# Other places in the on-chip memory for the split weights of a decoder trunk, with four tiles of each part in place of five

## The chip, the core and the metric

The kernel runs on one core of one Trainium2 chip. The metric is the device time of one execution, in microseconds; the span is the part of it that the profile covers. The engines are named as the profile names them: PE (TensorE, matrix products; PEld is its weight load), DVE (VectorE), ACT (ScalarE), POOL (GpSimd), SP (SyncE, which here issues nearly all transfers).

## What is computed

A trunk of two layers over 256 tokens of width 2048: first a pooling mixer, then 16-head attention, each followed by a gated feed-forward block of inner width 5632 with a causal convolution of three taps. Everything is float32, and nearly all of the arithmetic is `x @ W` with large matrices.

```python
for i in range(DEPTH):
    mod = cond @ w_ada[i] + b_ada[i]
    sh1, sc1, g1, sh2, sc2, g2 = jnp.split(mod, 6, axis=-1)
    h = modulate(rmsnorm(x, norm_g[i, 0]), sh1, sc1)
    y = pool_mixer(...) if i % N_MIXERS == 0 else moba_attention(h, w_qkv[li], w_o[li], rel_table)
    x = x + g1[:, None, :] * y
    h = modulate(rmsnorm(x, norm_g[i, 1]), sh2, sc2)
    x = x + g2[:, None, :] * conv_ffn(h, w_up[i], conv_w[i], conv_b[i], w_down[i])
return rmsnorm(x, final_g)
```

## The kernel before

**Steps and halves.** The matrices `w_up`, `w_down`, `w_qkv` and `w_o` are worked off in 328 steps (list `steps`). A step is a block of 512 rows by 512 columns: one transfer of 1 MB brings it into a raw tile of 128 partitions by 4 x 512 floats (`w_load`, five raw tiles). Each step has two halves of two 128-row blocks, 656 halves in all; half (133, 0) is the first half of step 133.

**The split.** Every half is split in two parts that PE can multiply in one pass (type float32r). ACT copies the raw half into the first part `hi` with rounding, then DVE writes the rest, raw minus `hi`, into the second part `lo` (`w_use`). The activations are split in the same way (tile `h` and the `act` and `o` tiles: first 256 columns rounded, next 256 the rest). A product then takes three matmuls of 256 columns for each 128 x 128 block of weights: `hi` with both parts of `h`, `lo` with the first. That is 24 matmuls for a half and 48 for a step; `v` alone multiplies the other way round, with the weights as the moving operand of 512 columns, 12 for a half.

**What sets how far the split runs ahead.** There are HB = 5 tiles for `hi` and 5 for `lo`. The split of a half is written into the program LAG = 3 halves ahead of its products: after it, the list `pending` is longer than LAG and `run_half` writes the products of the oldest half, with the side work that hangs on them.

```python
ac.activation(hi, src, AF.Copy)
ve.tensor_tensor(lo, src, hi.bitcast(F32), op=ALU.subtract)
pending.append((i, half) + ...)
if len(pending) > LAG:
    run_half()
```

A half can be split when its two tiles are free, that is when PE is through with the half that had them before. In the last step of every group, and in all steps of the first ten groups of layer 0 (which add each step's result to a tile in the on-chip memory, `home`), the products of both halves are written together, block by block, so both halves of the step stay occupied until its end.

**Order.** The first 200 of the loads and their uses are put in order on each engine by a scheduler, by priorities; from there on the engines run in the order in which the program was written. The conditioning products (`accs`, `acc`: DVE adds of raw tiles `ws`, `wa`) share DVE and the five raw tiles with the steps. At about 200 us the first step begins; what lies before is conditioning and the pooling mixer. Near 960 us and 1355 us a norm needs the whole of `x` before the next product can start.

**Places.** The tiles lie in the order in which the pools were made: constants, then `raw`, `hi`, `lo`, then the work pool. The tile `starts` is 48 floats long so that what follows begins 64 bytes past a multiple of 128. `h` begins at byte 36,864 of a partition, a multiple of 1024, and so do the tiles `act`, `o` and `pw`. Places modulo 1024 as built:

| tiles | before | after the change |
|---|---|---|
| raw, 5 of 8192 B | 960 each | 0 each |
| hi | 960 in all 5 | 64, 192, 320, 448 |
| lo | 960 in all 5 | 576, 704, 832, 960 |
| h, act, o, pw | 0 | 0 |

One 128-column block of a weight tile is 512 bytes, so from one column block to the next the place moves between 960 and 448 before.

Of the kernel before, what the change touches and what calls it, by code (L numbers as in the profile page):

```python
# [9 lines left out]
F32 = mybir.dt.float32  # L10
F32R = mybir.dt.float32r
# [6 lines left out]
P = 128  # L18
# [3 lines left out]
BUCKETS = 32  # L22
# [3 lines left out]
def bucket_starts():  # L26

    exact = BUCKETS // 2

    def bucket(n):  # L30
        if n < exact:
            return n
        big = exact + int(math.log(n / exact) / math.log(MAX_DIST / exact) * (BUCKETS - exact) + 1e-9)
        return min(big, BUCKETS - 1)

    of = [bucket(n) for n in range(4 * MAX_DIST)]
    return [next((n for n, b in enumerate(of) if b >= want), 1 << 20) for want in range(BUCKETS)]
# [19 lines left out]
def trunk(ctx: ExitStack, tc: tile.TileContext, x, c, norm_g, w_ada, b_ada, pool_w, pool_scale, w_qkv, w_o,  # L57
# [3 lines left out]
    _, S, D = x.shape  # L61
# [4 lines left out]
    H = rel_table.shape[1]  # L66
    NT = S // P
    SCALE = float(P) ** -0.5
    C = 512
# [3 lines left out]
    const = ctx.enter_context(tc.tile_pool(name="const", bufs=1))  # L73
    wp = ctx.enter_context(tc.tile_pool(name="wp", bufs=1))
# [2 lines left out]
    dram = ctx.enter_context(tc.tile_pool(name="dram", bufs=1, space=bass.MemoryType.DRAM))  # L77

    PE_BLOCKS = ((2, 5, 8, 11, 14), (3, 7, 11, 15), (2, 4, 6, 9, 11, 13, 15), (2, 5, 7, 10, 13, 15), ())
    RAW, HB, LAG, T4, PRIO = 5, 5, 3, 6, 1000  # L80

    def raw_tile(name):
        return wp.tile([P, 4 * C], F32, tag="raw", name=name, bufs=RAW)
# [4 lines left out]
    def aux(name):  # L88
        return psum.tile([P, C], F32, tag="aux", name=name, bufs=2)

    def wt(shape, tag, bufs, name, dt=F32):
        return work.tile(shape, dt, tag=tag, bufs=bufs, name=name)

    rel = wt([BUCKETS, H], "rel", 1, "rel")


    ident = const.tile([P, P], F32, name="ident")
# [570 lines left out]
    def bias_rows():  # L668

        starts = bucket_starts() + [1 << 20]  # L670
        st = const.tile([P, 48], F32, name="starts")[:, :BUCKETS + 1]
        for b, v in enumerate(starts):
            nc.gpsimd.memset(st[:, b:b + 1], float(v))
        nc.gpsimd.dma_start(rel, rel_table)
        e = wt([H, S + P], "t4", T4, "bias_e")
        nc.gpsimd.memset(e, NEG)
        for t in range(NT):
            ni = wt([P, 1], "st", 8, f"ni{t}", I32)
            nc.gpsimd.iota(ni, pattern=[[0, 1]], base=t * P, channel_multiplier=1)
            n = wt([P, 1], "st", 8, f"nf{t}")  # L680
            ve.tensor_copy(n, ni)
            ge = wt([P, BUCKETS + 1], "oh", 2, f"ge{t}")
            ve.tensor_scalar(ge, st, n, None, op0=ALU.is_le)
            oh = wt([P, BUCKETS + 1], "oh", 2, f"oh{t}")
            ve.tensor_tensor(oh[:, :BUCKETS], ge[:, :BUCKETS], ge[:, 1:], op=ALU.subtract)
            ps = aux(f"ohp{t}")
            pe.transpose(ps[:BUCKETS, :P], oh[:, :BUCKETS], ident)
            ohT = wt([BUCKETS, P], "vec", 4, f"ohT{t}")
            ve.tensor_copy(ohT, ps[:BUCKETS, :P])
            ps2 = aux(f"ohe{t}")  # L690
            pe.matmul(ps2[:H, :P], rel, ohT, start=True, stop=True)
            ve.tensor_copy(e[:, P - 1 + t * P:P - 1 + (t + 1) * P], ps2[:H, :P])
        nc.gpsimd.dma_start(bias_dram, e)
# [273 lines left out]
    def run_half():  # L967
        i, half, hi, lo = pending.pop(0)
        steps[i][3](half, hi, lo)
        if half == 1:  # L970
            for f in hooks.get(i, ()):
                f()
        h_next = ahead.pop(0) if ahead else None
        if h_next:
            h_next()
        else:
            run_tasks(2 if len(tasks) > MANY else 1)
        for _ in range(2):
            if folds:
                folds.pop(0)()  # L980
        for d in list(deferred):
            d[0] -= 1
            if d[0] <= 0:
                deferred.remove(d)
                d[1]()

    def w_use(i):
        def use(r):
            for half in range(2):
                hi = wp.tile([P, 2 * C], F32R, tag="hi", name=f"hi{i}_{half}", bufs=HB)  # L990
                lo = wp.tile([P, 2 * C], F32R, tag="lo", name=f"lo{i}_{half}", bufs=HB)
                src = r[:, half * 2 * C:(half + 1) * 2 * C]
                ac.activation(hi, src, AF.Copy)
                ve.tensor_tensor(lo, src, hi.bitcast(F32), op=ALU.subtract)
                pending.append((i, half) + tuple(t.rearrange("p (k c) -> p k c", k=2) for t in (hi, lo)))
                if len(pending) > LAG:
                    run_half()
        return use
# [47 lines left out]
    i = 0  # L1046
# [86 lines left out]
```

## Time and profile before

| | us |
|---|---|
| time, median of 3 runs (lowest to highest) | 2121.81 (2120.65 to 2122.86) |
| the profiled execution's own time | 2123.99 |
| its span | 2121.9 |
| PE busy in the span | 2066.2 |
| DVE busy | 1643.3 |
| ACT busy | 959.2 |

The profile is of one execution of its own, which took 2.18 us more than the median of the runs. Busy times overlap. A PE instruction counts as busy from its start to the modelled end of its pipeline, so instructions that follow each other overlap too, and the distance from start to start is what a matmul costs. Names of tiles stand without their numbers, so a row `lo<-w,hi` can be any half; which one it is follows from the engine's order. All compute instructions show line 50, a helper that records them; they are told apart by tiles.

### The profile page before, as it was taken

What the parts mean: (1) busy time and instruction counts of PE and PEld (TensorE: products, weight loads), DVE (VectorE), ACT (ScalarE), POOL (GpSimd) and SP (SyncE); (2) the same over time, 40 slices, a digit from 0 to 9 for tenths busy, and PEclk for the clock granted to TensorE, in tenths of its full rate; (3) what the DMA queues carried; (4) which work ended last, traced back from release to release, by engine and by line L of the source; (5) the groups of instructions that cost most, each with busy time, mean ns of one, the idle gap of its engine ahead of it and who ended that gap; (6) DMA issues with size and microseconds to landing.
All of it is one profiled execution on the core that took longest, in us unless ns stands there. A gap on an engine that the chain in (4) does not pass through costs nothing.

```text
span 2121.9 us, 38504 instructions
## 1 busy us (share of the span) xinstructions
PE 2066.2 (97%) x16292; PEld 1963.9 (93%) x16292; DVE 1643.3 (77%) x2023; ACT 959.2 (45%) x1206; POOL 12.0 (1%) x64
## 2 busy tenths in 40 slices
PE   6888999999999999999999999999999999999998
PEld 2435999999999999999999999999999999999998
DVE  6877799799879998997787878779775666556655
ACT  3113633566354445444544444445443454434443
POOL 1000000000000000000000000000000000000000
PEclk9889999999999999999999999999999999999999
DMA  9999999565998988896888888578765555555551
GB/s 357 333 348 345 335 334 320 198 197 181 348 332 292 358 314 308 304 326 213 307 294 310 295 310 302 190 259 282 278 233 179 190 179 189 196 180 188 192 179 60
DMA packets 236445, 558.78 MB, mean 263 GB/s; under 512 B 9272, under 2 KB 9592, under 8 KB 221680
## 3 DMA queue, kind: packets, MB, share of 16 engines
q1 hardware_dynamic: 234800, 553.17, 74.5%
q8 instruction: 127, 2.08, 0.4%
q0 software_dynamic: 896, 2.49, 0.4%
q10 hardware_dynamic: 576, 0.67, 0.1%
q14 instruction: 46, 0.38, 0.0%
HBM read 554.17 MB, written 2.12 MB: 262 GB/s over the span
## 4 chain that ended last, share of the span: by engine, by line
PE 95%; DVE 2%; DMA 2%; ACT 1%; issue 1%; ACTq 0%; SPq 0%; DVEq 0%
PE uv L50 24%; PE ug L50 23%; PE d L50 23%; PE k L50 4%; PE wo L50 4%; PE q L50 4%; PE v L50 4%; PE row L50 2%; PE pp L50 2%; PE mods L50 1%; DVE accs L50 1%; DVE pool_room L50 1%; DMA w<-in_w_up_dram 1%; DMA ws<-in_w_ada_dram 1%; PE sc L50 0%
## 5 line engine op out<-in xcount | busy, mean ns | idle before, releaser
L50 DVE TENSOR_TENSOR lo<-w,hi 128x1024 fp32r<-128x1024 f32 x656 | 793.9, 1222 | 320.7 <-ACT hi L50 319.7
L50 ACT ACTIVATE hi<-w 128x1024 fp32r<-128x1024 f32 x656 | 682.3, 1057 | 671.9 <-PE d L50 215.8
L50 PE MATMUL uv<-h,hi 128*128 128x256 f32 x2816 | 503.8, 281 | 4.2 <-ACT h L50 4.1
L50 PE MATMUL ug<-h,hi 128*128 128x256 f32 x2816 | 501.6, 280 | 0.2 <-ACT hi L50 0.2
L50 PE MATMUL d<-act,hi 128*128 128x256 f32 x2816 | 497.5, 280 | 0.0
L50 PEld LDWEIGHTS uv<-h,hi 128*128 128x128 f32 x2816 | 433.2, 189 | 5.2 <-ACT h L50 4.9
L50 PEld LDWEIGHTS ug<-h,hi 128*128 128x128 f32 x2816 | 431.3, 188 | 0.5 <-ACT hi L50 0.5
L50 PEld LDWEIGHTS d<-act,hi 128*128 128x128 f32 x2816 | 428.9, 187 | 0.0
L50 PE MATMUL uv<-h,lo 128*128 128x256 f32 x1408 | 394.1, 280 | 0.0
L50 PE MATMUL ug<-h,lo 128*128 128x256 f32 x1408 | 393.2, 279 | 0.0
L50 PE MATMUL d<-act,lo 128*128 128x256 f32 x1408 | 390.9, 279 | 0.0
L50 PEld LDWEIGHTS uv<-h,lo 128*128 128x128 f32 x1408 | 265.8, 189 | 0.0
L50 PEld LDWEIGHTS ug<-h,lo 128*128 128x128 f32 x1408 | 264.8, 188 | 0.0
L50 PEld LDWEIGHTS d<-act,lo 128*128 128x128 f32 x1408 | 263.5, 188 | 0.0
L50 DVE SCALAR_TENSOR_TENSOR acc<-wa,cond,acc 128x2048 f32<-128x2048 f32 x105 | 246.3, 2346 | 3.5 <-DMA wa<-in_w_ada_dram 3.3
L50 DVE SCALAR_TENSOR_TENSOR accs<-ws,cond,accs 128x512 f32<-128x512 f32 (+1 forms) x179 | 157.4, 882 | 23.3 <-DMA ws<-in_w_ada_dram 12.5
L50 PE MATMUL k<-h,hi 128*128 128x256 f32 x512 | 94.0, 285 | 1.1 <-ACT h L50 1.1
L50 PE MATMUL q<-h,hi 128*128 128x256 f32 x512 | 91.4, 280 | 0.0
L50 PE MATMUL wo<-o,hi 128*128 128x256 f32 x512 | 91.1, 280 | 0.0
L50 PE MATMUL row<-ws,cond 128*1 128x512 f32 x152 | 79.5, 647 | 10.3 <-DMA ws<-in_w_ada_dram 10.3
L50 PEld LDWEIGHTS k<-h,hi 128*128 128x128 f32 x512 | 79.9, 190 | 2.3 <-ACT h L50 1.4
L50 PE MATMUL v<-hi,h 128*128 128x512 f32 x256 | 80.4, 395 | 0.0
(157 smaller groups left out, 1751.7 us busy)
## 6 DMA issues: line engine op xcount, KB each, us to landing
w<-in_w_up_dram SPq DMA_DIRECT2D x176, 1024.0 KB, 5.2
wa<-in_w_ada_dram SPq DMA_DIRECT2D x112, 1024.0 KB, 6.0
w<-in_w_down_dram SPq DMA_DIRECT2D x88, 1024.0 KB, 5.1
ws<-in_w_ada_dram SPq DMA_DIRECT2D x56, 1024.0 KB, 9.0
w<-in_w_qkv_dram SPq DMA_DIRECT2D x48, 1024.0 KB, 5.9
ws<-in_w_ada_dram SPq DMA_DIRECT2D x48, 512.0 KB, 5.8
w<-in_w_o_dram SPq DMA_DIRECT2D x16, 1024.0 KB, 5.3
pw<-in_pool_w_dram SPq DMA_DIRECT2D x4, 1024.0 KB, 9.1
```

The lines of the kernel that those rows point to most:

```text
L50: ins = call(*args, **kwargs)
```

## The change

The tiles `hi` and `lo` get 32 floats more (4224 bytes instead of 4096), and the data lie 16 floats (64 bytes) into them. HB goes from 5 to 4 and LAG from 3 to 2. The small tile `rel` moves from the work pool to the constants, and `starts` is no longer padded; by that the raw tiles begin on a multiple of 1024, and the work pool keeps its places modulo 1024.

```diff
--- before.py
+++ after.py
@@ -77,7 +77,7 @@
     dram = ctx.enter_context(tc.tile_pool(name="dram", bufs=1, space=bass.MemoryType.DRAM))
 
     PE_BLOCKS = ((2, 5, 8, 11, 14), (3, 7, 11, 15), (2, 4, 6, 9, 11, 13, 15), (2, 5, 7, 10, 13, 15), ())
-    RAW, HB, LAG, T4, PRIO = 5, 5, 3, 6, 1000
+    RAW, HB, LAG, T4, PRIO = 5, 4, 2, 6, 1000
 
     def raw_tile(name):
         return wp.tile([P, 4 * C], F32, tag="raw", name=name, bufs=RAW)
@@ -90,8 +90,6 @@
 
     def wt(shape, tag, bufs, name, dt=F32):
         return work.tile(shape, dt, tag=tag, bufs=bufs, name=name)
-
-    rel = wt([BUCKETS, H], "rel", 1, "rel")
 
 
     ident = const.tile([P, P], F32, name="ident")
@@ -668,9 +666,10 @@
     def bias_rows():
 
         starts = bucket_starts() + [1 << 20]
-        st = const.tile([P, 48], F32, name="starts")[:, :BUCKETS + 1]
+        st = const.tile([P, BUCKETS + 1], F32, name="starts")
         for b, v in enumerate(starts):
             nc.gpsimd.memset(st[:, b:b + 1], float(v))
+        rel = const.tile([BUCKETS, H + 8], F32, name="rel")[:, :H]
         nc.gpsimd.dma_start(rel, rel_table)
         e = wt([H, S + P], "t4", T4, "bias_e")
         nc.gpsimd.memset(e, NEG)
@@ -987,8 +986,9 @@
     def w_use(i):
         def use(r):
             for half in range(2):
-                hi = wp.tile([P, 2 * C], F32R, tag="hi", name=f"hi{i}_{half}", bufs=HB)
-                lo = wp.tile([P, 2 * C], F32R, tag="lo", name=f"lo{i}_{half}", bufs=HB)
+
+                hi, lo = (wp.tile([P, 2 * C + 32], F32R, tag=w, name=f"{w}{i}_{half}", bufs=HB)[:, 16:16 + 2 * C]
+                          for w in ("hi", "lo"))
                 src = r[:, half * 2 * C:(half + 1) * 2 * C]
                 ac.activation(hi, src, AF.Copy)
                 ve.tensor_tensor(lo, src, hi.bitcast(F32), op=ALU.subtract)
```

The same instructions are issued on every engine; SP's and POOL's stand in the same order as before. On ACT, DVE and, in the scheduled part, PE the order changes, as at these places.

**DVE in the up products of layer 0, steps 13 to 15 (`home`: a product's result added to its tile; `accs`: conditioning).** Before, the piece from the second split of step 13 to the first of step 15 reads on DVE:

```order
L50 TENSOR_TENSOR lo13_1_1927<-w13_1720,hi13_1_1926 128x1024
L50 TENSOR_TENSOR lo14_0_1942<-w14_1831,hi14_0_1941 128x1024
L50 TENSOR_TENSOR home0_1178<-home0_1178,ug0_0_0_1930 128x512
L50 SCALAR_TENSOR_TENSOR accs_207<-ws3_2_3_1867,cond_95,accs_207 128x1024 x2
L50 TENSOR_TENSOR home0_1178<-home0_1178,ug0_0_1_1931 128x512
L50 TENSOR_TENSOR lo14_1_1994<-w14_1831,hi14_1_1993 128x1024
L50 TENSOR_TENSOR lo15_0_2009<-w15_1872,hi15_0_2008 128x1024
```

Now the piece from the first split of step 13 to the second of step 14 reads on DVE:

```order
L50 TENSOR_TENSOR lo13_0_1923<-w13_1768,hi13_0_1922 128x1024
L50 TENSOR_TENSOR lo13_1_1931<-w13_1768,hi13_1_1930 128x1024
L50 TENSOR_TENSOR home0_1174<-home0_1174,ug0_0_0_1926 128x512
L50 SCALAR_TENSOR_TENSOR accs_206<-ws3_2_3_1915,cond_94,accs_206 128x1024 x2
L50 TENSOR_TENSOR home0_1174<-home0_1174,ug0_0_1_1927 128x512
L50 TENSOR_TENSOR lo14_0_1990<-w14_1855,hi14_0_1989 128x1024
L50 TENSOR_TENSOR lo14_1_1998<-w14_1855,hi14_1_1997 128x1024
```

The pair of splits between two steps' additions was the second half of one step and the first of the next, and is now both halves of one step.

**DVE at the first norm of layer 1 (`ht` and `h1_0` make the new activations; step 132 is the first of the attention).** Before, the activations 4 to 7 of the norm stand like this on DVE:

```order
L50 SCALAR_TENSOR_TENSOR ht10_4_9921<-xT_101,gsc_115,rrow_9901 128x256
L50 SCALAR_TENSOR_TENSOR ht10_5_9924<-xT_101,gsc_115,rrow_9901 128x256
L50 SCALAR_TENSOR_TENSOR h1_0_9904<-ht10_4_9921,mod_114,h1_0_9904 128x256
L50 SCALAR_TENSOR_TENSOR h1_0_9904<-ht10_5_9924,mod_114,h1_0_9904 128x256
L50 TENSOR_TENSOR lo133_1_9930<-w133_9546,hi133_1_9929 128x1024
L50 TENSOR_TENSOR lo134_0_9962<-w134_9619,hi134_0_9961 128x1024
L50 SCALAR_TENSOR_TENSOR ht10_6_9989<-xT_101,gsc_115,rrow_9901 128x256
L50 SCALAR_TENSOR_TENSOR ht10_7_9992<-xT_101,gsc_115,rrow_9901 128x256
L50 SCALAR_TENSOR_TENSOR h1_0_9904<-ht10_6_9989,mod_114,h1_0_9904 128x256
L50 SCALAR_TENSOR_TENSOR h1_0_9904<-ht10_7_9992,mod_114,h1_0_9904 128x256
L50 TENSOR_TENSOR lo134_1_9998<-w134_9619,hi134_1_9997 128x1024
```

Now the same activations stand like this on DVE:

```order
L50 SCALAR_TENSOR_TENSOR ht10_4_9915<-xT_100,gsc_114,rrow_9895 128x256
L50 SCALAR_TENSOR_TENSOR ht10_5_9918<-xT_100,gsc_114,rrow_9895 128x256
L50 SCALAR_TENSOR_TENSOR h1_0_9898<-ht10_4_9915,mod_113,h1_0_9898 128x256
L50 SCALAR_TENSOR_TENSOR h1_0_9898<-ht10_5_9918,mod_113,h1_0_9898 128x256
L50 TENSOR_TENSOR lo133_0_9926<-w133_9605,hi133_0_9925 128x1024
L50 TENSOR_TENSOR lo133_1_9956<-w133_9605,hi133_1_9955 128x1024
L50 SCALAR_TENSOR_TENSOR ht10_6_9983<-xT_100,gsc_114,rrow_9895 128x256
L50 SCALAR_TENSOR_TENSOR ht10_7_9986<-xT_100,gsc_114,rrow_9895 128x256
L50 SCALAR_TENSOR_TENSOR h1_0_9898<-ht10_6_9983,mod_113,h1_0_9898 128x256
L50 SCALAR_TENSOR_TENSOR h1_0_9898<-ht10_7_9986,mod_113,h1_0_9898 128x256
L50 TENSOR_TENSOR lo134_0_9994<-w134_9675,hi134_0_9993 128x1024
```

Half (133, 0) was split ahead of the norm and now stands behind its first six activations, where (133, 1) stood; (133, 1) stands where (134, 0) stood.

**DVE and PE in the first down product with a residual, steps 82 to 85 (`xT<-dy`: residuals of an earlier product; `gate`, `val`: side work of the up product; `acc`: conditioning).** DVE behind the split of (83, 1), before, runs to the split of (84, 1) through these rows:

```order
L50 SCALAR_TENSOR_TENSOR gate0_7_6461<-ug0_7_0_6187,cw00_396,gate0_7_6461 128x254
L50 SCALAR_TENSOR_TENSOR acc1_1_6368<-wa1_1_4_6570,cond_95,acc1_1_6368 128x2048
L50 SCALAR_TENSOR_TENSOR gate0_7_6461<-ug0_7_1_6188,cw01_400,gate0_7_6461 128x255
L50 SCALAR_TENSOR_TENSOR xT_101<-dy0_5542,mod_114,xT_101 128x256 x4
L50 SCALAR_TENSOR_TENSOR xT_101<-dy1_5606,mod_114,xT_101 128x256 x4
L50 SCALAR_TENSOR_TENSOR xT_101<-dy2_5670,mod_114,xT_101 128x256
L50 TENSOR_TENSOR lo84_0_6644<-w84_6498,hi84_0_6643 128x1024
L50 SCALAR_TENSOR_TENSOR xT_101<-dy2_5670,mod_114,xT_101 128x256
L50 TENSOR_TENSOR lo84_1_6676<-w84_6498,hi84_1_6675 128x1024
```

Now the rows behind the split of (83, 1) on DVE are these:

```order
L50 SCALAR_TENSOR_TENSOR acc1_1_6392<-wa1_1_4_6596,cond_94,acc1_1_6392 128x2048
L50 SCALAR_TENSOR_TENSOR gate0_7_6452<-ug0_7_1_6184,cw00_395,gate0_7_6452 128x254
L50 SCALAR_TENSOR_TENSOR xT_100<-dy0_5533,mod_113,xT_100 128x256 x4
L50 SCALAR_TENSOR_TENSOR xT_100<-dy1_5597,mod_113,xT_100 128x256 x4
L50 SCALAR_TENSOR_TENSOR xT_100<-dy2_5661,mod_113,xT_100 128x256 x4
L50 SCALAR_TENSOR_TENSOR xT_100<-dy3_5913,mod_113,xT_100 128x256 x2
L50 TENSOR_TENSOR lo84_0_6672<-w84_6525,hi84_0_6671 128x1024
L50 SCALAR_TENSOR_TENSOR xT_100<-dy3_5913,mod_113,xT_100 128x256
L50 TENSOR_TENSOR val0_7_6170<-gate0_7_6452,val0_7_6170 128x1024
L50 SCALAR_TENSOR_TENSOR xT_100<-dy3_5913,mod_113,xT_100 128x256
L50 SCALAR_TENSOR_TENSOR acc1_1_6392<-wa1_1_5_6666,cond_94,acc1_1_6392 128x2048
L50 TENSOR_TENSOR lo84_1_6704<-w84_6525,hi84_1_6703 128x1024
```

Between the splits of (83, 1) and (84, 1) there are now 16 residuals instead of 10, two conditioning adds instead of one, one `val` product more and one `gate` add less. PE at the first matmul of half (83, 1) before, which is followed by the first of (84, 0):

```order
L50 MATMUL d0_1_0_0_6469<-act0_5_6048,hi83_1_6605 128x256 x2
L50 MATMUL d0_1_0_1_6470<-act0_5_6048,hi83_1_6605 128x256 x2
L50 MATMUL d0_1_1_0_6535<-act0_5_6048,hi84_0_6643 128x256 x2
L50 MATMUL d0_1_1_1_6536<-act0_5_6048,hi84_0_6643 128x256 x2
L50 MATMUL d0_1_0_0_6469<-act0_5_6048,lo83_1_6606 128x256
L50 MATMUL d0_1_0_0_6469<-act0_5_6048,hi83_1_6605 128x256 x2
L50 MATMUL d0_1_2_0_6609<-act0_4_6079,hi82_0_6500 128x256 x2
```

PE now at the first matmul of half (84, 0):

```order
L50 MATMUL d0_1_2_1_6606<-act0_4_6075,hi82_1_6560 128x256 x2
L50 MATMUL d0_1_2_1_6606<-act0_4_6075,lo82_1_6561 128x256
L50 MATMUL d0_1_1_0_6531<-act0_5_6042,hi84_0_6671 128x256 x2
L50 MATMUL d0_1_1_1_6532<-act0_5_6042,hi84_0_6671 128x256 x2
L50 MATMUL d0_1_2_0_6605<-act0_5_6042,hi85_0_6740 128x256 x2
L50 MATMUL d0_1_2_1_6606<-act0_5_6042,hi85_0_6740 128x256 x2
L50 MATMUL d0_1_1_0_6531<-act0_5_6042,lo84_0_6672 128x256
```

All matmuls of step 82 now stand ahead of step 84; counted over the whole order, the first `lo` matmul of half (84, 1) comes 30 matmuls later than before.

## Rows read from the trace of the kernel before

**Rows 1.** The page's head and its busy times (us, share of the span, instructions)

```profile
span 2121.9 us, 38504 instructions
...
PE 2066.2 (97%) x16292; PEld 1963.9 (93%) x16292; DVE 1643.3 (77%) x2023; ACT 959.2 (45%) x1206; POOL 12.0 (1%) x64
```

**Rows 2.** The page's chain that ended last, shares by line

```profile
PE uv L50 24%; PE ug L50 23%; PE d L50 23%; PE k L50 4%; PE wo L50 4%; PE q L50 4%; PE v L50 4%; PE row L50 2%; PE pp L50 2%; PE mods L50 1%; DVE accs L50 1%; DVE pool_room L50 1%; DMA w<-in_w_up_dram 1%; DMA ws<-in_w_ada_dram 1%; PE sc L50 0%
```

**Rows 3.** Busy time by windows: PE, PEld, DVE, ACT, POOL, clock, DMA, GB/s

```profile
60.00:120.00 60.00, 54.03 (x196) 26.04 (x195) 47.35 (x86) 9.06 (x14) 2.57 (x6) 0.89 0.93 333
280.00:310.00 30.00, 30.00 (x257) 30.00 (x256) 29.15 (x31) 11.79 (x12) 0.00 (x0) 1.00 0.98 341
400.00:500.00 100.00, 100.00 (x851) 100.00 (x850) 92.17 (x144) 65.74 (x87) 0.00 (x0) 1.00 0.57 184
660.00:700.00 40.00, 40.00 (x342) 40.00 (x341) 39.07 (x50) 18.52 (x20) 0.00 (x0) 1.00 0.86 314
1600.00:1700.00 100.00, 100.00 (x851) 100.00 (x850) 58.92 (x71) 42.27 (x47) 0.00 (x0) 1.00 0.58 190
```

**Rows 4.** The chain in order of time: start us, us, what

```profile
286.28 5.65 PE ug L50 x48
...
971.10 5.65 PE q L50 x48
976.75 5.60 PE v L50 x24
```

**Rows 5.** Timeline of PE at three places: start us, us, instructions

```profile
686.35 0.28 PE L50 MATMUL d<-act,lo 128*128 128x256 f32 x1
...
1000.16 0.40 PE L50 MATMUL k<-h,hi 128*128 128x256 f32 x2
...
1000.51 0.40 PE L50 MATMUL k<-h,hi 128*128 128x256 f32 x2
...
1000.87 0.40 PE L50 MATMUL k<-h,hi 128*128 128x256 f32 x2
...
1038.56 1.05 PE L50 MATMUL sc<-k,q 128*128 128x128 f32 x8
```

**Rows 6.** Groups by form: busy us, mean ns of one, idle before

```profile
L50 DVE TENSOR_TENSOR lo<-w,hi 128x1024 fp32r<-128x1024 f32 x656 | 793.9, 1222 | 320.7 <-ACT hi L50 319.7
L50 ACT ACTIVATE hi<-w 128x1024 fp32r<-128x1024 f32 x656 | 682.3, 1057 | 671.9 <-PE d L50 215.8 <-PE ug L50 176.9 <-PE uv L50 173.5
...
L50 DVE TENSOR_TENSOR val<-gate,val 128x1024 f32<-128x1024 f32 x22 | 26.8, 1220 | 1.5 <-ACT gate L50 1.4
```

**Rows 7.** DMA issues: count, KB each, median us to landing

```profile
ws<-in_w_ada_dram SPq DMA_DIRECT2D x56, 1024.0 KB, 9.0
...
pw<-in_pool_w_dram SPq DMA_DIRECT2D x4, 1024.0 KB, 9.1
```

**Rows 8.** Waits: who for whom, us in total, times, longest

```profile
DVE lo L50 <- ACT hi L50: 319.7, 252, 4.5
ACT hi L50 <- PE d L50: 215.8, 119, 5.1
```

**Rows 9.** Timeline of DVE at three places

```profile
281.60 2.36 DVE L50 TENSOR_TENSOR lo<-w,hi 128x1024 fp32r<-128x1024 f32 x2
...
677.19 3.64 DVE L50 SCALAR_TENSOR_TENSOR xT<-dy,mod,xT 128x256 f32<-128x256 f32 x9
...
682.28 1.22 DVE L50 TENSOR_TENSOR lo<-w,hi 128x1024 fp32r<-128x1024 f32 x1
...
686.18 2.35 DVE L50 SCALAR_TENSOR_TENSOR acc<-wa,cond,acc 128x2048 f32<-128x2048 f32 x1
...
968.36 2.36 DVE L50 TENSOR_TENSOR lo<-w,hi 128x1024 fp32r<-128x1024 f32 x2 [0.46 <-ACT hi L50]
```

**Rows 10.** Busy time by windows in the opening, same columns as group 3

```profile
4.00:8.00 4.00, 0.97 (x3) 0.46 (x3) 4.00 (x10) 0.97 (x1) 0.71 (x2) 1.00 1.02 423
...
44.00:48.00 4.00, 4.00 (x27) 2.72 (x28) 2.73 (x5) 2.23 (x5) 0.00 (x0) 1.00 1.05 387
```

## Prediction

> **What bounds the kernel now.** I read the busy times first: of a span of 2121.9 us PE is busy for 97%, DVE for 77%, ACT for 45% [rows 1]. The reader is to see there that only PE is near the span; but the other engines can still set the end in a stretch, so the chain of waits is next. Followed back from the last instruction it is nearly all PE: `uv`, `ug` and `d` (up and down products) with 24, 23 and 23%, the four attention products with 4% each, while the DMAs and DVE's conditioning that come up in it have about 1% each [rows 2]. Third, the windows show where PE isn't full: between 60 and 120 us it works for 54 of 60 us at a granted clock of 0.89, with the DMA engines at 0.93 [rows 3]. The opening, up to about 200 us, is paced by transfers. From there on PE is full at clock 1.00 in all the stretches shown, and the stretches of 100 us at 400 and at 1600 both hold 851 matmuls, though DVE is busy for 92.17 us in the one and 58.92 in the other [rows 3]. So PE's pace doesn't depend on what DVE and ACT do beside it: 48 matmuls of 256 columns take 5.65 us, 0.1177 each, and 24 of 512 columns 5.60, 0.2333 each [rows 4]. The 624 halves other than those of `v` hold 624 x 24 = 14,976 matmuls of the first kind, 1763 us: that term is what a change can move.
>
> **The parts of the change.** It has two: other places, and one tile and one half less of look-ahead. The first acts on every matmul if it acts at all, so I begin there.
>
> *Places and PE.* Instructions and sizes stay the same. PE loads 128-column blocks of `hi` and `lo` as weights and streams `h`, `act` or `o`. Before, neighbouring blocks of a tile already alternate between 960 and 448 modulo 1024, which are 512 apart. If the distance of 512 mattered, the matmuls on one block would be slower than those on the next. The `k` products at 1000.16, 1000.51 and 1000.87 us go from block to block, and their starts are 0.35, 0.36 apart, three matmuls each, at 0.118 [rows 5]. In `v` the roles are changed (`hi` and `lo` stream, `h` is the weight), and a column costs 0.2333/512 = 0.456 ns there against 0.1177/256 = 0.460 in the others [rows 4]. So four of the places that occur, in both roles, have one rate, and the phase between `hi` and `lo` doesn't show in it. The four new places 64, 192, 320 and 704, with their partners, are odd multiples of 64 like the old ones, and no row has them. I take 0; both ends are priced under the rivals.
>
> *Places, ACT and DVE.* 656 splits cost 1057 ns on ACT and 1222 on DVE [rows 6]. The nearest row with other places is `val<-gate,val`, the same shape with two reads and a write in the work pool: 1220 ns [rows 6]. Between the two there are 2 ns a half, and the spare time of DVE covers them; without cover 656 x 0.002 = 1.3 us. I take 0.
>
> *Places and DMA.* The raw tiles go from 960 to 0. A megabyte into `pw`, which already lies at 0, lands in 9.1 us, one into a raw tile (`ws`) in 9.0 [rows 7]. I take 0, which hides nothing, since both ends are measured; a gain in the opening is a rival. `starts` and `rel` cost nothing: the same small transfer and fills on POOL, in the same order, and they lie under the opening's transfers; POOL is busy for 12 us in all [rows 1].
>
> *Four tiles, LAG 2.* No instruction is added. A split waits until PE has left the tiles, and with four tiles that moment comes one half later: 24 x 0.1177 = 2.83 us. Such waits are common: ACT waited 119 times for the `d` matmuls alone, 215.8 us, and DVE's `lo` 252 times for `hi`, 319.7 us [rows 8]. They cost nothing now since PE has work ahead; the question is where the `lo` of a half would end after PE's need of it. Behind a late split there stand, in DVE's order, the side work of the products and the next split; PE waits for both. I looked at the places with the least slack.
>
> - Up products of layer 0. The pair of splits that ended at 281.60 + 2.36 = 283.96 us was the second half of step 13 and the first of step 14; in the new order both halves of step 14 must be ready when its products begin, at 286.28 [rows 4, 9]. If the pair that stands in this place now is that of step 14, it ends 2.3 us before it is needed. DVE is busy for 29.15 of 30 us here [rows 3], so the margin is small, but positive: 0.
> - First norm of layer 1. Half (133, 0) goes behind six activations of the norm, and takes the place of (133, 1). The pair in that place ended at 968.36 + 2.36 = 970.72 [rows 9], and `q` of step 132 began at 971.10 [rows 4], with 5.65 us of products ahead of step 133. So there is no wait: 0.
> - Steps 83 to 85, where DVE is busy for 39.07 of 40 us [rows 3]. The `lo` of half (84, 1) ended at 682.28 + 1.22 = 683.50 [rows 9] and PE first needed it at 686.35 [rows 5]: margin 2.85. Now DVE has more ahead of it: six residuals at 3.64/9 = 0.40 are 2.4 us, one `acc` 2.35 [rows 9], one `val` 1.22 [rows 6], one `gate` add less, about 0.4 (taken as a residual's): +5.5. PE needs it 30 matmuls later: 30 x 0.1177 = 3.5. The margin falls to 2.85 - 5.5 + 3.5 = 0.8 us. If the splits ahead are in addition held by their tiles for up to 2.83, it is 0.8 - 2.8 = -2.0. So this place costs 0 to 2.0 us; I take the middle, 1.0, as neither end is nearer to a row.
> - Layer 2 from 1400 us on has DVE at 59 of 100 us [rows 3], a slack of some 41 us in which a shift of 2.83 is lost: 0.
>
> *Sum.* The profiled execution took 2123.99 us, its span and 2.09 around it, and lies 2.18 above the median of the runs. 2123.99 + 0 (PE's pace) + 0 (ACT, DVE, DMA) + 1.0 (steps 83 to 85) = 2124.99; less 2.18 it is **2122.8 us** on the scale of the runs. That is 0.05% above 2121.81 and below the 0.2%, 4.2 us, that a measurement of this kernel can tell from no change.
>
> **Rivals.**
>
> *Starvation (the other side).* The mechanism of steps 83 to 85, but at all places where DVE is nearly full: a split comes 2.83 us later, DVE has nothing to do meanwhile, and can't make up for it. It decides where the sum of DVE's work between two needed splits, with that idle time, is longer than PE's products between them. For it: DVE has only 0.85 us free in 30 at 280 us and 0.93 in 40 at 660 [rows 3]. Against it: before 960 us there is more slack elsewhere (7.8 in 100 at 400 us), and PE did not wait once for DVE in those stretches. I count five such dense stretches, the two of [rows 3] and three like them (from 340, 450 and 906 us on); if each loses one half's time, 5 x 2.83 = 14 us: about 2136. From 2128 on I count it as this case.
>
> *The old places held PE's pace.* 256 columns might take less than 0.1177. The nearest row is `sc`, whose operands lie elsewhere and whose matmuls are of another kind (128 columns): eight end 1.05 us after the first began and the last takes some 0.28 as a single one does, so (1.05 - 0.28)/7 = 0.110 from start to start [rows 5]. Taken as a bound for the pace: (0.1177 - 0.110) x 14,976 = 115 us less, about 2008. It decides only if 320 beside 832 is quicker than 960 beside 448, which the even pace over `k`'s blocks speaks against [rows 5]. DVE, at 92.17 of 100 us [rows 3], would nearly become the bound.
>
> The Trainium skill, "TensorE: Matmul & The Clock Gate", section "Wait — 56ns, not 53.3ns?", gives the start-to-start time of warm matmuls as the columns over 2.4 GHz and about 2.5 ns, measured: 215.7 ns at 512 columns. That would be 109 ns at 256, an estimate by the page; the rows here, 117.7 and 233.3, are both 1.08 times as long, so something that grows with the columns takes the difference, and if the places did, the change could win some 130 us by the page. The trace can't tell whether they do; that both lengths are off by one factor, in both roles, fits a cause that isn't the place of the weights.
>
> *The new places slow PE.* The same mechanism with the other sign: 64, 192, 320 or 704 collide with `h` at 0 or with a tile that ACT or DVE writes. No row has them, so I bound it by the same 0.0077 us a matmul: up to about 2237. Against it: pace equal at DVE 92 and 59 of 100 [rows 3], so writes into the memory don't slow PE's reads here.
>
> *Landings at 0 are quicker.* The opening is bound by transfers for some 190 us. `x` landed at 423 GB/s in the window 4 to 8 us, the `ws` tiles at 387 in 44 to 48 [rows 10]; if all of the difference were the place, the opening would take 190 x (1 - 387/423) = 16 us less, about 2106. Against it: the two durations for one megabyte, 9.0 and 9.1 [rows 7].
>
> The Trainium skill, "DMA: Bandwidth & Descriptors", section "How a descriptor splits into AXI transactions", says that a transaction has to start at a 256-byte boundary; a start at 960 costs one transaction more than one at 0. It would speak for this rival if it held for the writing side, which [rows 7] don't show.
>
> **How the numbers follow.** Forecast, 2119 to 2127: 0.58. The pace rests on 851 matmuls per 100 us in two stretches, and the margins are worked out at the three tightest places. Starvation, 2128 to 2136: 0.20, since DVE's slack is under 1 us in two stretches and waits for tiles are frequent. Old places held the pace: 0.09. New places slow it: 0.06. Landings: 0.05. The remaining 0.02 are gains or losses of a few us in the opening, where the scheduler's order changes. The range goes from the forecast's lower part to the end of starvation, **2117 to 2136**, and leaves out the three cases of places, 0.20. Faster by over 0.2%: 0.09 + 0.05 = 0.14. Slower: starvation 0.20, slower pace 0.06, and 0.04 from the upper end of the forecast and the opening: 0.30. Within 0.2%: 0.56.
>
> **What would show it.** Right: 851 matmuls per 100 us from 400 and from 1600 us; 5.65 us for 48 `q` matmuls; ACT `hi` and DVE `lo` at 1057 and 1222 ns; ACT's waits for PE longer in sum than now, with PE's busy time unchanged; a gap of PE of at most 2 us near 686 us. Wrong: a pace other than 0.1177 between steps, which would show in every window from 200 us on (places); gaps of PE that end with DVE's `lo` in the dense stretches (starvation); an opening whose first step begins more than 4 us earlier or later (landings, scheduler). The forecast falls above all if the places do matter in a way that the four old ones don't show.

## The result, and the profile after the change

The changed kernel takes 2074.85 us in the median (2071.65 to 2076.08), against 2122.34 for the kernel before; the ratio is 0.977, with an interval of 0.975 to 0.979. It is faster by some 48 us, where the forecast was no change. Its page gives the span and PE's busy time like this:

```profile
span 2074.3 us, 38497 instructions
...
PE 2013.0 (97%) x16292; PEld 1907.9 (92%) x16292; DVE 1641.4 (79%) x2023; ACT 960.2 (46%) x1206; POOL 12.0 (1%) x64
```

DVE and ACT work as long as before, and the share of PE is the same 97% [rows 1]; what became shorter is the time that PE spends on the same 16,292 matmuls. The windows of [rows 3] from 280 us on, of the kernel after (PE, PEld, DVE, ACT, POOL, clock, DMA share, GB/s):

```profile
280.00:310.00 30.00, 30.00 (x267) 30.00 (x266) 28.20 (x32) 10.07 (x10) 0.00 (x0) 1.00 0.96 342
400.00:500.00 100.00, 100.00 (x885) 100.00 (x884) 96.91 (x149) 68.43 (x91) 0.00 (x0) 1.00 0.59 197
660.00:700.00 40.00, 37.26 (x322) 36.66 (x322) 38.44 (x39) 16.98 (x16) 0.00 (x0) 1.00 0.83 311
1600.00:1700.00 100.00, 100.00 (x885) 100.00 (x884) 63.81 (x77) 50.95 (x57) 0.00 (x0) 1.00 0.59 194
```

Read the count behind PE's time: 885 matmuls in 100 us at clock 1.00 where it was 851. So one starts some 113 ns after the other in place of 117.5 (a little more, since a window also counts those begun just before it). A busy share can't show this, since PE was full in both. But from 660 to 700 us PE isn't full any more: 37.26 of 40 us, where it was 40.00 [rows 3]. The chain that ended last, in order of time, shows that the pace isn't one number (start, duration, matmuls of 256 columns):

```profile
1192.39 5.44 PE q L50 x48
...
1346.00 5.66 PE ug L50 x48
...
1362.75 5.44 PE ug L50 x48
...
2050.41 5.66 PE d L50 x48
```

A step takes 5.44 us in most places, but at some, as the step at 1346 us soon after the norm, still 5.66, which is the old 5.65 of [rows 4]. There are two levels, 113 to 114 ns and 117 to 119, and next to nothing between them. Over all starts of the matmuls on `hi` and `lo` less than 150 ns apart the mean is 113.7 ns after and 117.8 before.

The other work kept its durations. The groups by form (busy us, mean ns of one, idle before), which answer to [rows 6]:

```profile
L50 DVE TENSOR_TENSOR lo<-w,hi 128x1024 fp32r<-128x1024 f32 x656 | 790.9, 1221 | 260.0 <-ACT hi L50 259.1
L50 ACT ACTIVATE hi<-w 128x1024 fp32r<-128x1024 f32 x656 | 683.2, 1059 | 630.5 <-PE d L50 185.6 <-PE ug L50 152.3 <-PE uv L50 141.9
L50 PE MATMUL d<-act,lo 128*128 128x256 f32 x1408 | 387.4, 277 | 4.0 <-DVE lo L50 4.0
```

The last of them is new: PE waits for `lo`, 4.0 us in all. On PE's timeline the waits of the `d` products stand in brackets, with what ended them:

```profile
669.28 0.39 PE L50 MATMUL d<-act,lo 128*128 128x256 f32 x1 [1.25 <-DVE lo L50]
...
672.99 0.74 PE L50 MATMUL d<-act,hi 128*128 128x256 f32 x4 [0.61 <-ACT hi L50]
...
674.61 0.38 PE L50 MATMUL d<-act,lo 128*128 128x256 f32 x1 [0.88 <-DVE lo L50]
...
885.40 0.46 PE L50 MATMUL d<-act,lo 128*128 128x256 f32 x1 [1.87 <-DVE lo L50]
```

After the longest of them the granted clock fell, and for some 3 us matmuls started 213 ns apart, as at the lower of the two levels of the clock (1.2 GHz). The window around it:

```profile
880.00:890.00 10.00, 8.13 (x58) 7.93 (x57) 9.93 (x12) 4.19 (x5) 0.00 (x0) 0.83 0.79 241
```

The difference adds up. I took the starts of all matmuls on `hi` and `lo`. 14,976 of 256 columns at 117.77 - 113.68 = 4.09 ns less are 61.3 us. I call it a break where two starts lie more than 12 ns further apart than 115 ns (232 for `v`), whatever stands between: a wait, other matmuls, the lower clock. What lies above 115 ns in the breaks grew from 56.5 to 69.2 us, 12.7 more; 7.7 more in the steps 80 to 131, 7.0 more in the attention (`q`, `k`, `v`), and some 2 less in the rest. The first step began 0.9 us later, at 201.6. That makes 61.3 - 12.7 - 0.9 = 47.7 us, and the last of these matmuls began 47.6 us earlier.

### The profile page after: what moved, and what is told of

The parts are those of the page before. It is cut to its first block, busy times and chain, and to the rows that moved or that the text cites. A ratio compares the mean times of both kernels' runs of the same rounds, so it can differ in the third digit from the quotient of the medians.

```text
span 2074.3 us, 38497 instructions
## 1 busy us (share of the span) xinstructions
PE 2013.0 (97%) x16292; PEld 1907.9 (92%) x16292; DVE 1641.4 (79%) x2023; ACT 960.2 (46%) x1206; POOL 12.0 (1%) x64
## 5 line engine op out<-in xcount | busy, mean ns | idle before, releaser
L50 DVE TENSOR_TENSOR lo<-w,hi 128x1024 fp32r<-128x1024 f32 x656 | 790.9, 1221 | 260.0 <-ACT hi L50 259.1
L50 ACT ACTIVATE hi<-w 128x1024 fp32r<-128x1024 f32 x656 | 683.2, 1059 | 630.5 <-PE d L50 185.6
L50 PE MATMUL uv<-h,hi 128*128 128x256 f32 x2816 | 485.1, 278 | 3.8 <-ACT h L50 3.8
L50 PE MATMUL d<-act,hi 128*128 128x256 f32 x2816 | 482.0, 277 | 0.6 <-ACT hi L50 0.6
L50 PE MATMUL ug<-h,hi 128*128 128x256 f32 x2816 | 481.8, 276 | 0.0
L50 PEld LDWEIGHTS uv<-h,hi 128*128 128x128 f32 x2816 | 426.6, 189 | 4.5 <-ACT h L50 4.1
L50 PEld LDWEIGHTS ug<-h,hi 128*128 128x128 f32 x2816 | 424.0, 188 | 0.0
L50 PE MATMUL uv<-h,lo 128*128 128x256 f32 x1408 | 387.9, 277 | 0.0
L50 PE MATMUL ug<-h,lo 128*128 128x256 f32 x1408 | 386.3, 276 | 0.0
```

Source lines behind the costliest of these rows:

```text
L50: ins = call(*args, **kwargs)
```

## The experiments

The theory after the first look: the places set PE's pace, and the four tiles cost some 10 us. The rivals: the fewer tiles and the shorter look-ahead make the gain; or, of the places, the offset of 512 between `hi` and `lo` does, or the step of 128 from tile to tile. In the changed kernel a series of matmuls that was slow behind a break became fast, nearly always, where the weights passed from a tile at 192 or 448 to one at 64 or 320. So I call a place by its class, the remainder modulo 256: 960, 192, 448 and 704 are in class 192, and 64, 320, 576 and 832 in class 64. The streamed tiles `h`, `act` and `o` lie in class 0.

**Four tiles, the old places.**

```diff
+hi = wp.tile([P, 1280], F32R, tag="hi", ...)[:, 240:240 + 2 * C]
+lo = wp.tile([P, 1280], F32R, tag="lo", ...)[:, 240:240 + 2 * C]
```

> Four tiles of each part and LAG 2, as in the change, but all eight tiles at 960 modulo 1024 as before. Theory (the places set the pace of PE): every 256-column matmul starts 118 ns after the one before, as in the kernel before, and the time is 2122 to 2135 us, the gaps of PE costing 0 to 12 us more than before. Rival (fewer tiles and the shorter look-ahead make the gain): 113 to 114 ns and about 2075 us.

2133.67 us, ratio 1.005 (1.003 to 1.007). Windows:

```profile
400.00:500.00 100.00, 100.00 (x852) 100.00 (x851) 93.23 (x143) 63.95 (x85) 0.00 (x0) 1.00 0.52 180
...
1600.00:1700.00 100.00, 100.00 (x851) 100.00 (x851) 59.16 (x70) 42.45 (x45) 0.00 (x0) 1.00 0.55 190
```

The pace is the old one and the time some 10 us longer; PE's breaks add up to 66.6 us, 10.1 more than before; 3.7 of them lie in the steps 80 to 131 and 8.1 in `q`, `k` and `v`. So the edit of HB and LAG alone makes the kernel slower, and all of the gain is in the places. The raw tiles lie at 0 here as after the change, so they have no part in the pace.

**The offset of 512 alone.**

```diff
+hi = wp.tile([P, 1280], F32R, tag="hi", ...)[:, 16:16 + 2 * C]
+lo = wp.tile([P, 1280], F32R, tag="lo", ...)[:, 144:144 + 2 * C]
```

> Four tiles, LAG 2; every hi tile at 64 and every lo tile at 576 modulo 1024: the offset of 512 alone, with no step from tile to tile. Theory of the offset: 113 to 114 ns a matmul, about 2075 us. Rival, theory of the step (PE goes to the faster pace when the weights change from a tile at 192 to one at 64 modulo 256, and keeps it): no such change, 118 ns, 2122 to 2135 us.

2095.45 us, ratio 0.987 (0.984 to 0.989): neither of the two. Windows:

```profile
400.00:500.00 100.00, 100.00 (x851) 100.00 (x851) 93.23 (x143) 64.50 (x86) 0.00 (x0) 1.00 0.52 182
800.00:900.00 100.00, 100.00 (x885) 100.00 (x884) 93.14 (x103) 50.50 (x59) 0.00 (x0) 1.00 0.87 309
```

The same program has either level for hundreds of microseconds: slow from 248 to 671 us, fast from 782 to 948. Each change of level stands at a break: 16 small `mods` matmuls of the conditioning at 246 us, two small `modc` matmuls at 671 and again at 781. So a level is held, and a break can end it.

**The step of 128 alone.**

```diff
+hi = wp.tile([P, 1056], F32R, tag="hi", ...)[:, 16:16 + 2 * C]
+lo = wp.tile([P, 1312], F32R, tag="lo", ...)[:, 144:144 + 2 * C]
```

By the larger `lo` tiles (their step is 5248 bytes) both parts lie at 64, 192, 320 and 448.

> Four tiles, LAG 2; the places 64, 192, 320, 448 modulo 1024 for hi and the same four for lo: the step of 128 from tile to tile alone, without the offset of 512. Theory of the step: 113 to 114 ns, 2072 to 2080 us. Theory of the offset: 118 ns, 2122 to 2135 us.

2073.28 us, ratio 0.977 (0.975 to 0.979), and in the window where the run with the offset had 851 matmuls there are 885:

```profile
400.00:500.00 100.00, 100.00 (x885) 100.00 (x884) 97.06 (x150) 67.72 (x91) 0.00 (x0) 1.00 0.55 190
```

The step gives the whole gain and the offset isn't needed for it.

**The same tiles on multiples of 128.**

```diff
+hi = wp.tile([P, 1056], F32R, tag="hi", ...)[:, 0:0 + 2 * C]
+lo = wp.tile([P, 1056], F32R, tag="lo", ...)[:, 0:0 + 2 * C]
```

> The changed kernel with all eight tiles 64 bytes earlier: 0, 128, 256, 384 and 512, 640, 768, 896 modulo 1024. If only the differences between tiles matter: 113 to 114 ns and about 2075 us, as in the changed kernel. If the 64 bytes past a multiple of 128 matter by themselves: another pace, slower than 114 ns in all windows; at 118 ns about 2130 us, and more if it is slower than both levels seen so far.

2152.53 us, ratio 1.014 (1.012 to 1.016): a third pace, 119.2 ns on average.

```profile
400.00:500.00 100.00, 100.00 (x842) 100.00 (x841) 88.66 (x137) 64.09 (x85) 0.00 (x0) 1.00 0.54 188
...
1600.00:1700.00 100.00, 100.00 (x841) 100.00 (x840) 52.62 (x64) 38.57 (x39) 0.00 (x0) 1.00 0.55 190
```

Steps of 128 don't help here; the 64 bytes past a multiple of 128 are a condition.

**No step and no offset, and steps of 256.** First all eight tiles at 64:

```diff
+hi = wp.tile([P, 1280], F32R, tag="hi", ...)[:, 16:16 + 2 * C]
+lo = wp.tile([P, 1280], F32R, tag="lo", ...)[:, 16:16 + 2 * C]
```

> Four tiles, LAG 2, all eight tiles at 64 modulo 1024: neither step nor offset. Theory (PE has two levels, 113 to 114 and 118 ns; a pause of PE draws one of them and it is held while the places stay in one class): a mixture in pieces that begin and end at pauses, as in the run with the offset alone, 2085 to 2115 us. Rival (the offset of 512 gave that mixture): 118 ns in nearly all of it, 2125 to 2138 us.

2091.55 us, ratio 0.984 (0.982 to 0.986). Then places 64, 320, 576 and 832, all in class 64:

```diff
+hi = wp.tile([P, 1088], F32R, tag="hi", ...)[:, 16:16 + 2 * C]
+lo = wp.tile([P, 1088], F32R, tag="lo", ...)[:, 16:16 + 2 * C]
```

> Four tiles, LAG 2; places 64, 320, 576, 832 for hi and for lo: steps of 256 in place of 128, all in one class modulo 256. Theory (only a change of class modulo 256, which steps of 128 make, brings PE to the faster level): a mixture that changes at pauses alone, 2085 to 2135 us. Rival (any step from tile to tile does it): 113 to 114 ns nearly throughout, 2070 to 2080 us.

2090.05 us, ratio 0.984 (0.982 to 0.987). The windows of the run with all tiles at 64, and behind them those of the run with steps of 256:

```profile
400.00:500.00 100.00, 100.00 (x852) 100.00 (x851) 93.23 (x144) 63.72 (x85) 0.00 (x0) 1.00 0.53 182
...
1600.00:1700.00 100.00, 100.00 (x885) 100.00 (x884) 61.77 (x74) 46.68 (x51) 0.00 (x0) 1.00 0.57 195
```

```profile
400.00:500.00 100.00, 100.00 (x851) 100.00 (x851) 93.05 (x143) 65.74 (x87) 0.00 (x0) 1.00 0.55 190
...
1600.00:1700.00 100.00, 100.00 (x885) 100.00 (x884) 60.67 (x72) 46.54 (x51) 0.00 (x0) 1.00 0.56 192
```

Both are the mixture of the run with the offset. So neither the offset nor a step inside one class does anything beyond what class 64 gives by itself; a step between the classes does. I counted it over all series of matmuls without a break, cut also where the class changes (six matmuls or more; fast or slow by the median distance):

```
                       behind a break or v    at 192 -> 64 from slow    at 64 -> 192 from slow    fast level lost
                          fast / slow            to fast / stays           to fast / stays         at a change
before (all 960)            2 / 39
four tiles, all 960         2 / 44
offset of 512 (all 64)     28 / 21
all 64                     24 / 24
steps of 256               22 / 25
after                      14 / 29                11 / 1                     0 / 3                 0 of 531
step of 128 alone          14 / 31                10 / 3                     0 / 2                 0 of 530
```

Read down the first column: in class 192 a series begins slow nearly always, in class 64 about every second one does (after the change 0 fast and 19 slow in class 192, 14 and 10 in class 64). Read across: passing to class 64 brings a slow series to the fast level in 21 of 25 cases, passing to class 192 never, and the fast level, once there, is kept in both classes until the next break.

**Four tiles with the longer look-ahead.**

```diff
-    RAW, HB, LAG, T4, PRIO = 5, 4, 2, 6, 1000
+    RAW, HB, LAG, T4, PRIO = 5, 4, 3, 6, 1000
```

> The changed kernel with LAG 3 in place of 2, four tiles kept, the same places. Theory (the gaps of PE at steps 84 and 123 come from DVE's order, in which the splits stand one half later): without them 8 to 12 us less, 2062 to 2068 us. Rival (they come from the four tiles, whatever the order): 2070 to 2080 us, or more if DVE now waits in its queue ahead of the products' side work.

2075.49 us, ratio 0.977 (0.975 to 0.979), the same as the change. PE's breaks are 70.2 us. In DVE's order 555 of 656 splits stand where they stood before (319 with the change), and nothing is won in the sum. The waits at steps 84 and 123 did go, and in `q`, `k` and `v` the breaks are 25.6 us (31.8 with the change, 24.8 before). But the down products of the steps 80 to 131 lose 7.4 us, at other steps (8.4 with the change, 0.7 before, the norm left out), and the two norms more: from the last product before a norm to the first one behind it PE takes 9.4 and 9.8 us, with the change 6.0 and 5.5. DVE at the first of them:

```profile
933.83 1.23 DVE L50 TENSOR_TENSOR lo<-w,hi 128x1024 fp32r<-128x1024 f32 x1 [3.07 <-ACT hi L50]
934.97 1.65 DVE L50 SCALAR_TENSOR_TENSOR xT<-d,mod,xT 128x256 f32<-128x256 f32 x4
```

A split that must wait for its tile (ACT's part of it waited 3.88 us for PE's `d` products) now stands ahead of the norm's last residuals, and holds them up; at the second norm it waits 3.54 us. So the theory was right on where those waits came from and wrong on the time: with four tiles either look-ahead costs some 10 us or more, and what costs is the number of tiles, as the runs with five show below.

**Five tiles at two places.** The tiles get tags of their own; the data of the first `hi` tile begin 64 bytes into it, and another 128 bytes stand ahead of the third (`HPAD` is the room for it, and 64 bytes behind the last tile):

```diff
-    RAW, HB, LAG, T4, PRIO = 5, 4, 2, 6, 1000
+    RAW, HB, LAG, T4, PRIO = 5, 5, 3, 6, 1000
+    HAT = {(n, w): 16 if (n, w) == (0, "hi") else 32 if (n, w) == (2, "hi") else 0 for n in range(HB) for w in ("hi", "lo")}
...
+                n = next(slot) % HB
+                hi, lo = (wp.tile([P, 2 * C + HPAD[n, w]], F32R, tag=f"{w}{n}", ...)[:, HAT[n, w]:HAT[n, w] + 2 * C]
```

> Five tiles and LAG 3 as before the change, tiles 0 and 1 of both parts at 64 and tiles 2 to 4 at 192 modulo 1024, so that one change from 192 to 64 comes in every five halves; act and o lie at 256 modulo 1024 by it. Theory (that change sets the level, and the four tiles cost some 10 us): 113 to 114 ns nearly throughout, 2056 to 2068 us, faster than the changed kernel. Rival (all four places are needed, or act and o must lie at a multiple of 1024): pieces at 118 ns, 2085 to 2125 us.

2060.27 us, ratio 0.970 (0.968 to 0.972): faster than both kernels. Its windows:

```profile
400.00:500.00 100.00, 100.00 (x885) 100.00 (x884) 97.61 (x151) 67.83 (x91) 0.00 (x0) 1.00 0.56 191
...
660.00:700.00 40.00, 38.93 (x332) 38.34 (x332) 36.34 (x36) 16.24 (x16) 0.00 (x0) 1.00 0.83 317
800.00:900.00 100.00, 100.00 (x883) 100.00 (x883) 96.77 (x105) 46.94 (x53) 0.00 (x0) 1.00 0.89 322
```

The pace is that of the change (113.75 ns on average) and the breaks are down to 56.9 us, which is the sum of before. In 13 of 17 cases the passage from 192 to 64 ended a slow series.

**Five tiles, all at 64.** As the last one, without the 128 bytes (they go behind the last tile, so `act` and `o` stay where they were):

```diff
+    HAT = {(n, w): 16 if (n, w) == (0, "hi") else 0 for n in range(HB) for w in ("hi", "lo")}
```

> Five tiles and LAG 3, all ten tiles at 64 modulo 1024, act and o at 256: the places of the run with all tiles at 64 without the smaller number of tiles. Theory (four tiles cost some 10 us through gaps of PE, the places do the rest): 118 and 113 ns in pieces between pauses as there, and 2075 to 2095 us by how the pieces fall. Rival (act and o at 256, not the change of class, gave the run with two places its pace): 113 to 114 ns nearly throughout, about 2060 us.

2083.71 us (2076.36 to 2084.03), ratio 0.980 (0.978 to 0.981); the trace is of the execution of 2076.36. Again slow, then fast:

```profile
400.00:500.00 100.00, 100.00 (x852) 100.00 (x851) 93.56 (x145) 64.26 (x85) 0.00 (x0) 1.00 0.57 186
...
1600.00:1700.00 100.00, 100.00 (x885) 100.00 (x884) 63.99 (x76) 51.23 (x58) 0.00 (x0) 1.00 0.59 191
```

With eight tiles at these places it was 2091.55; the breaks are 54.6 us here and 70.6 there. That `act` and `o` lie at 256 doesn't give the pace.

**`hi` at 64, `lo` at 192.** Five tiles of 4096 bytes; a fill of 128 bytes stands between the two parts and one of 64 behind `lo`, and `rel` is 64 bytes longer, so that the raw tiles and `hi` begin at 64 and `act` and `o` at 256:

```diff
+rel = const.tile([BUCKETS, H + 24], F32, name="rel")[:, :H]
...
+hi = wp.tile([P, 2 * C], F32R, tag="hi", ..., bufs=HB)
+if "b" not in gap:
+    gap["b"] = wp.tile([P, 32], F32, tag="gap", ...)
...
+lo = wp.tile([P, 2 * C], F32R, tag="lo", ..., bufs=HB)
+if "e" not in gap:
+    gap["e"] = wp.tile([P, 16], F32, tag="gape", ...)
...
```

> Five tiles and LAG 3; every hi tile at 64 and every lo tile at 192 modulo 1024, act and o at 256. No tile's place moves from half to half, but the weights go from 192 to 64 after each lo matmul. Theory (any change of the weights from 192 to 64 brings PE to the faster level): fast within a few matmuls after every pause, hardly any at 118 ns, 2050 to 2060 us. Rival (the class must hold for a half or more before the level can change): a mixture or another pace, 2075 to 2125 us.

2060.87 us (2057.42 to 2064.25), ratio 0.970 (0.968 to 0.972), just above the 2060 that was expected as the most; the pace is as expected. Only 213 of the starts lie from 116 to 130 ns (1358 with two places), and the mean is 113.4:

```profile
400.00:500.00 100.00, 100.00 (x885) 100.00 (x884) 97.60 (x152) 67.83 (x90) 0.00 (x0) 1.00 0.58 190
...
1600.00:1700.00 100.00, 100.00 (x884) 100.00 (x884) 66.56 (x81) 52.87 (x61) 0.00 (x0) 1.00 0.59 191
```

The passage need not come from tile to tile, it works within a block too. What it saves against the run with two places, 1145 x 4 ns = 5 us, isn't seen in the medians (the two executions traced differ by it: 2057.42 and 2062.24 us).

**Moving the streamed tiles in place of the weights.** In the kernel before, a fill of 128 bytes behind `lo` moves `act` and `o` to 128; `h` stays at 0:

```diff
 lo = wp.tile([P, 2 * C], F32R, tag="lo", name=f"lo{i}_{half}", bufs=HB)
+if not gap:
+    gap.append(wp.tile([P, 32], F32, tag="gap", name="gap", bufs=1))
...
```

> The kernel before the change (five tiles, LAG 3, all at 960 modulo 1024) with everything of the work pool 128 bytes further, so that act and o, which stream against the weights in the down and output products, lie at 128 modulo 1024, and h stays at 0. Theory (what counts is the distance of the weights from the streamed tile): going from the up to the down products is then a change of class, 118 ns up to the first down product and the faster level at many places from there, 2065 to 2100 us. Rival (the place of the weights counts by itself): 118 ns nearly everywhere, 2118 to 2128 us.

2113.11 us, ratio 0.995 (0.993 to 0.996): between the two ranges and in neither. The windows of a stretch of `d` products and of up products behind it:

```profile
1580.00:1620.00 40.00, 40.00 (x356) 40.00 (x355) 22.50 (x27) 15.26 (x15) 0.00 (x0) 1.00 0.56 191
1640.00:1680.00 40.00, 40.00 (x342) 40.00 (x342) 25.54 (x32) 20.22 (x24) 0.00 (x0) 1.00 0.54 185
```

The weights are at 960 all the time. In the `d` products, where the distance to the streamed tile is now 960 - 128, in class 64, 64% of the starts are at the fast level, in the up products none, before none in either. So the place of the weights by itself isn't all; the distance between the weights and the streamed tile fits what is seen. But the passage is not the one of the other runs: of six `d` stretches two became fast at their beginning, three only at a break within them and one not at all, and at each return to the up products the fast level was lost without a break (three of three), which a passage from tile to tile never did.

The other side of it, the kernel with all weights on multiples of 128 and a fill of 64 bytes behind `lo`:

```diff
 lo = wp.tile([P, 1056], F32R, tag="lo", name=f"lo{i}_{half}", bufs=HB)[:, 0:0 + 2 * C]
+if not gap:
+    gap.append(wp.tile([P, 16], F32, tag="gap", name="gap", bufs=1))
...
```

> The kernel with all weight tiles on multiples of 128, with everything of the work pool 64 bytes further: act and o at 64 modulo 1024, h at 0. Theory of the distance: the down and output products (d, wo) run at 113 to 118 ns, the others at 119 to 120 as before; about 2135 to 2148 us. Rival (the place of the weights counts by itself): 119 to 120 ns in d and wo too, 2149 to 2159 us.

2127.29 us in one run. Up products and `d` products:

```profile
1400.00:1440.00 40.00, 40.00 (x338) 40.00 (x338) 29.56 (x32) 17.81 (x21) 0.00 (x0) 1.00 0.80 287
...
1860.00:1900.00 40.00, 40.00 (x356) 40.00 (x355) 22.32 (x26) 15.06 (x15) 0.00 (x0) 1.00 0.53 185
```

`d` runs at 113.8 ns and `wo` at 114.3, all others at 119.2 or a little more, as in the run without the fill. Of the two, the theory of the distance holds, and the gain, (119.2 - 113.8) x 4992 = 27 us of 2152.53, was larger than I had put it. That it is the difference of the two places that counts, and not some other relation of them, rests on these two runs and isn't shown beyond them.

## Why the prediction was wrong

**The step that failed** is "Places and PE", its value 0. It took four places for a sample of the eight: 960 and 448, as weights and as streamed tiles, showed one rate [rows 4, 5], and from that followed that the phase between `hi` and `lo` doesn't show in it. But 960 and 448 are in one class modulo 256, and the runs show that the class is what divides the levels. (The new places are also six and not the four that it lists: 64, 192, 320, 576, 704 and 832, of which 192 and 704 are in the old class.) The equal pace from block to block was no evidence either, since a level, once there, is held over blocks, and was held in the trace of before nearly from end to end. The steadiness from which I took that there is nothing to gain was that of the slower of two levels.

**The rival that came true** is "the old places held PE's pace". It had a chance of 0.09. Its size was taken from `sc`, 0.0077 us a matmul and 115 us; measured are 0.0041 and 61.3. The rule that I gave the mechanism, 320 beside 832, is wrong: it isn't `hi` beside `lo` but the class of the distance to the streamed tile, and the passage from one class to the other.

The Trainium skill, "TensorE: Matmul & The Clock Gate", section "Wait — 56ns, not 53.3ns?", from which the prediction had worked out 109 ns at 256 columns, an estimate, spoke for this rival by its direction. No run here reaches that figure: the faster level is 113 to 114.

**Places of ACT, DVE and the raw tiles:** right. 1059 and 1221 ns against 1057 and 1222 [rows 6]. The first step began at 201.6 us against 200.7, so the landings didn't shorten the opening (over all the kernels' traces it began between 197.4 and 204.3), though the median of the `ws` transfers fell from 9.0 [rows 7] to 7.6 us; that of `pw` is 9.0, it was 9.1:

```profile
ws<-in_w_ada_dram SPq DMA_DIRECT2D x56, 1024.0 KB, 7.6
...
pw<-in_pool_w_dram SPq DMA_DIRECT2D x4, 1024.0 KB, 9.0
```

**Four tiles, LAG 2:** mis-sized. The place was right: PE waits at step 84 for DVE's `lo`. The sum of this term was 1.0 us; it measured 10.1 at the old pace (the run with four tiles at the old places) and 12.7 at the new one. At the old pace, for which the term was worked out, the breaks of steps 84 to 86 are 2.9 us, where I had reckoned with at most 2.0, and most of the rest, 8.1, lies in the attention, which I had not looked at. In the trace after the change 7.7 lie in the steps 80 to 131, since one wait drew others behind it (in steps 84 and 86) and a second place, step 123 at 885 us, cost a wait of 1.87 and some of the clock; and 7.0 lie in the attention. The up products of layer 0, which I had priced at 0, lose nothing (breaks of over 0.15 us: 5.6 us against 7.0 before). The rival of starvation had 14 us, about the right size, for five stretches of which two show it (those from 660 and from 906 us on, by the times of before). That the shorter look-ahead of LAG would move the splits was a cause I had not kept apart from the tiles: with LAG 3 PE waits at other places, the norms above all, and the time is the same.

## What to carry to other kernels

When PE is the bound and full, count the matmuls in a window and work out the time from start to start; a busy share of 100% hides a pace that is 4% too slow. If that time is above what the shortest rows of the same trace suggest, move the weights against the streamed tile, in both classes and on purpose, and try it by itself: `hi` at 64 and `lo` at 192, with a fill of 128 bytes between them, gave here 2060.87 us with five tiles, less than the change. And a place that shows one rate everywhere is one sample, however many rows it has.

## What the hardware showed that I had not expected

A float32r matmul of 256 columns, back to back with its own weight load, has one of three paces here, by the place of the weights less that of the streamed tile: 119.2 ns on average at multiples of 128, and 117 to 119 or 113 to 114 at 64 past one. Between these two levels the last break decides, and the class: at 192 modulo 256 nearly all series begin slow (39 of 41 before), at 64 about half. A passage from 192 to 64 brings the fast level in most cases (48 of 58 over the runs after, with the step alone, with LAG 3 and with two places). Neither DVE's load nor the transfers show in it: with five tiles at two places 100 us hold 885 matmuls with DVE at 97.61 us and the DMA engines at 0.56, and 883 with the DMA engines at 0.89.

Why a level is held, and what in the loading of weights and the streaming of columns makes two of them, is open: the records have a start and a modelled end of each matmul, and nothing of the reads from memory. `v`, with 512 columns and the roles changed, shows no two such levels: the medians of its distances are 229 to 233 ns over all runs. Open is also why the passage by another streamed tile loses the fast level where the passage by another weight tile keeps it.
